# Value products of the last neighbourhood heads spread over other projections, and the high parts of the dilated values' operand copied into residue order

## The chip, the cores and the metric

The kernel runs on one core of a Trainium2 chip. The core has a matrix engine (TensorE, PE in the profile, its weight loads PEld), a vector engine (VectorE, DVE), a scalar engine (ScalarE, ACT), GpSimd (POOL) and SyncE (SP), which work side by side and wait for each other by semaphores; each runs its own instructions in the order in which they stand in the program. Matmul results go into PSUM, here eight banks of 128 partitions x 512 floats. The metric is the device time of one execution in microseconds (us); lower is better.

## What is computed

One layer of an encoder: a half-step feed-forward block, a mixing block, and a second half-step feed-forward block, each between two RMS norms, for 512 tokens of 1024 channels in float32. The change lies in the mixing block:

```
proj = h @ w_in[l]
qa, ka, va, qb, kb, vb, gate_a, gate_b = jnp.split(proj, splits, axis=-1)
ya = _neighbourhood_attention(qa, ka, va, na_rpb[l]) @ w_branch_a[l]
yb = _dilated_mixture(qb, kb, vb, slopes) @ w_branch_b[l]
merged = jax.nn.sigmoid(gate_a) * ya + jax.nn.sigmoid(gate_b) * yb
x = x + _rmsnorm(merged @ w_out[l], mix_post_g[l])
```

The neighbourhood attention has 8 heads of 64 channels, each query looking at a window of rows and columns of a 64-column grid. The dilated mixture has three groups of 4 heads: group 0 looks at neighbours at distance 1, group 1 at every 4th token, group 2 at every 16th. The three results of a head are mixed by their log-sum-exps.

## The kernel before

All products are made in three matmuls of reduced-precision parts: an operand is split into a high part (a cast, on ACT, line 116) and a low part (a subtraction, on DVE, line 117), and `mm3` (lines 207 to 209) sums high x high, high x low and low x high. `hn_hi` and `hn_lo` hold the normalised input of the mixing block, transposed: channels in the partitions, in NK = 8 chunks of 128, and 512 tokens in the free dimension. Weights come from HBM in pieces, are split likewise, and `take()` hands out the next piece. `bank()` gives a PSUM bank out of eight, `unit()` an SBUF buffer of 128 x 512 out of 46; who asks for one waits until its last user has gone.

The stretch of the mixing block in question runs so. `pair` makes the projections of the queries and of the keys of one pair of heads: 24 matmuls into a bank each, 5.7 us. After each projection it calls `step`, which takes the next entry from the list `pend` and issues it: the attention of earlier heads is interleaved with the projections in this way. There are four pairs of neighbourhood heads (`na_use`), then six pairs of dilated heads (`g_use`, pairs 0 and 1 of group 0, 2 and 3 of group 1, 4 and 5 of group 2). A pair of neighbourhood heads has three kinds of step: `sc` (scores of both heads, their minimum and exponential, lines 1109, 1116 and 1121), `na_tr` (transposes of one head's probabilities and their split, line 1143), and `na_pv` (value product of one head, line 1170, and then in `attend` a copy on ACT and an addition on DVE, line 1188, which read the bank; line 1186 is the copy). The table `plan` in `na_use` says which of them go together in one entry of `pend`: each inner tuple is one entry, so one entry is issued per projection. The last line of `plan`, that of the last pair, has eight entries, issued in pairs 1 to 4 of the dilated heads.

A pair of dilated heads is made into operands by `qk_parts` (lines 969 to 976, and 116, 117): of the queries a scaled high part on ACT (969) and a low part on DVE (970), of the keys a cast on ACT and a subtraction on DVE for each half, and copies to the other half of the partitions on DVE (975) and ACT (976). Scores of group 0 are made by `scores`, those of groups 1 and 2 by `scores_narrow` (lines 1081, 1085 and 1089): two matmuls to a bank, an addition of a table and two reductions on DVE, exponentials on ACT.

After the six pairs, `v_far` makes the values of groups 1 and 2: four accumulators of a bank each, over all eight chunks; for each chunk and each n of four, `mm3` with 128 tokens as the stationary operand and 512 columns of weight as the moving one. The 128 tokens are those of one residue modulo 4: `seen(1, .)` is a view of the chunk, every fourth token of 512, so PE's weight load reads it with a stride of 4. After every second chunk it calls `step` (twice after chunk 5), which issues the narrow scores that are left. Then `v_near` makes the values of group 0 (four products of 24 matmuls with 256 columns) and then come the gates.

The function `recopy` (line 990) is a plain copy on DVE or ACT; before the change it is used by the neighbourhood values, which are made from copies in another order of tokens, and by `v_near` for the tokens at the two ends.

A scheduler turns the code into one row of instructions for each engine; what is independent can stand in another order than in the code, by its estimates. An engine then keeps to its row.

Of the kernel before, what the change touches and what calls it, by code (L numbers as in the profile page):

```python
# [13 lines left out]
F32R = mybir.dt.float32r  # L14
# [6 lines left out]
P = 128  # L21
T = 512
D = 1024
NK = D // P
# [22 lines left out]
def block_kernel(ctx, tc, x, gains, weights, rpb_near, rpb_all, alibi0, alibi12, out):  # L47
    nc = tc.nc
# [12 lines left out]
    def unit(dt=F32, name="u"):  # L61
        return up.tile([P, 512], dt, tag="u", name=name)
# [9 lines left out]
    def bank(name="ps"):  # L72
        return pp.tile([P, 512], F32, tag="ps", name=name)
# [17 lines left out]
    hn_hi, hn_lo = Rows(), Rows()  # L91
# [88 lines left out]
    def cut(w, c, n):  # L180

        return [a[c // 512][:, c % 512:c % 512 + n] for a in w]

    def take(ahead=True):
        w = pieces.pop(state["take"])
        state["take"] += 1
        if ahead:
            fill(NPIECE - 1)
        return w
# [11 lines left out]
    def step(n=1):  # L201
        for _ in range(n):
            if pend:
                pend.popleft()()

    def mm3(o, sh, sl, mh, ml, start, stop, **kw):
        nc.tensor.matmul(o, sh, mh, start=start, stop=False, **kw)  # L207
        nc.tensor.matmul(o, sh, ml, start=False, stop=False, **kw)  # L208
        nc.tensor.matmul(o, sl, mh, start=False, stop=stop, **kw)  # L209
# [701 lines left out]
    def seen(kind, ap):  # L911

        if kind == "na":
            return ap.rearrange("p (r c) -> p c r", r=8)
        if kind == 0:
            return ap
        return ap.rearrange("p (i c) -> p c i", c=4)
# [24 lines left out]
    def shaped(dst, view):  # L942
        sh = view.shape
        if len(sh) == 2:
            return dst
        if len(sh) == 3:
            return dst.rearrange("p (a b) -> p a b", a=sh[1])
        return dst.rearrange("p (a b c) -> p a b c", a=sh[1], b=sh[2])

    def qk_parts(kind, pq, pk):  # L950


        if kind not in (1, 2):
            qh, ql, kh, kl = [unit(F32R, n) for n in "qqkk"]
            v = seen(kind, pq)
            qo = shaped(qh, v)
            nc.scalar.mul(qo, v, 0.125)
            nc.vector.scalar_tensor_tensor(shaped(ql, v), v, 0.125, qo.bitcast(F32), op0=ALU.mult, op1=ALU.subtract)
            for cols, v in order_k(kind, pk):
                split(shaped(kh[:, cols], v), shaped(kl[:, cols], v), v)  # L960
            return qh, ql, kh, kl
        heads = []
        for par in range(2):
            own = slice(par * 64, par * 64 + 64)
            other = slice(64 - par * 64, 128 - par * 64)
            q, kh, kl = unit(F32R, "q"), unit(F32R, "k"), unit(F32R, "k")
            v = seen(kind, pq[own])
            qo, qx = shaped(q[own], v), shaped(q[other], v)
            nc.scalar.mul(qo, v, 0.125)
            nc.vector.scalar_tensor_tensor(qx, v, 0.125, qo.bitcast(F32), op0=ALU.mult, op1=ALU.subtract)  # L970
            v = seen(kind, pk[own])
            for i, u in enumerate((kh, kl)):
                part = v[:, 2 * i:2 * i + 2]
                split(shaped(u[own, :256], part), shaped(u[own, 256:], part), part)
            nc.vector.tensor_copy(kh[other], kh[own].bitcast(F32))
            nc.scalar.copy(kl[other], kl[own].bitcast(F32))
            heads.append((q, kh, kl))
        return heads

    def v_parts(ps):  # L980
        v = unit(F32R)
        v4 = v.rearrange("p (h s d) -> p h s d", h=4, s=2)
        split(v4[:, :, 0, :], v4[:, :, 1, :], ps.rearrange("p (h d) -> p h d", h=4))
        return v4

    def recopy(dst, src, eng):
        if eng is nc.scalar:
            nc.scalar.copy(dst, src.bitcast(F32))
        else:
            nc.vector.tensor_copy(dst, src.bitcast(F32))  # L990
# [27 lines left out]
    def v_far():  # L1018

        acc = [bank() for _ in range(4)]  # L1020
        for k in range(NK):
            if k % 2 == 0:
                w = take()
            parts = [seen(1, a[:, k, :]) for a in (hn_hi, hn_lo)]
            for n in range(4):
                mm3(acc[n], parts[0][:, n], parts[1][:, n], *cut(w, (k % 2) * 512, 512), k == 0, k == NK - 1)
            if k % 2:
                step(2 if k == 5 else 1)
        vv = [[], []]
        for n in range(4):  # L1030
            for i in range(2):
                vv[i].append(v_parts(acc[n][:, i * 256:(i + 1) * 256]))
        return vv
# [196 lines left out]
    def mixing(g):  # L1230
# [9 lines left out]
        def load_tables(us, n, src):  # L1240
            def one(i):
                u = unit(name="table")
                nc.sync.dma_start(u, src[:, i * 512:(i + 1) * 512])
                us.append(u)
            for i in range(n):
                loads.append(lambda i=i: one(i))
# [16 lines left out]
        def na_sc(parts, h):  # L1263
            s4 = [sp.tile([P, 4, 1, 2], F32, tag="nast", name="nast", bufs=4) for _ in range(2)]
            pr = scores(parts, [table_of(na_tab[h // 2], n) for n in range(2)],
                        [lambda i, t=t: t[:, i, 0] for t in s4])
            for n in range(2):
                rc = sp.tile([P, 4], F32, tag="narc", name="narc", bufs=4)
                nc.vector.reciprocal(rc, s4[n][:, :, 0, 1])
                scale_probs(True, pr[n], lambda i: rc[:, i:i + 1])  # L1270
                hold["p", h + n] = pr[n]
# [7 lines left out]
        def na_use(p, pq, pk):  # L1279
            if p < 3:  # L1280
                load_tables(na_tab[p + 1], 3, bias_f[:, (p + 1) * 1536:(p + 2) * 1536])
            parts = qk_parts("na", pq, pk)
            sc = lambda: na_sc(parts, 2 * p)
            plan = (((sc,), (), ((na_tr, 0),)),
                    (((na_tr, 1),), (sc,), ((na_pv, 0),), ((na_pv, 1), (na_tr, 2))),
                    (((na_tr, 3),), (sc,)),
                    (((na_pv, 2),), ((na_pv, 3), (na_tr, 4)), ((na_tr, 5),), (sc,), ((na_pv, 4),),
                     ((na_pv, 5), (na_tr, 6)), ((na_tr, 7),), ((na_pv, 6), (na_pv, 7))))
            for group in plan[p]:
                pend.append(lambda group=group: [f() if callable(f) else f[0](f[1]) for f in group])  # L1290

# [51 lines left out]
        load_tables(na_tab[0], 3, bias_f[:, 0:1536])  # L1343
        v_na = v_proj_na()
        first_pairs(na_use, (0, 2), lambda: next(v_na))
        vva += next(v_na)
        g_post, g_pre = gain(g), gain(g + 1)
        pair(na_use, 2, 1)
        pair(na_use, 3, 1)
        load_tables(g_tab[0], 3, alibi0[:, :1536])  # L1350
        load_tables(g_tab[1], 3, alibi0[:, 1536:])
        load_tables(g_tab[2], 1, alibi12[:, :512])
        load_tables(g_tab[3], 1, alibi12[:, 512:])
        for j in range(6):
            pair(g_use, j, 1)
        pend.append(lambda: joint(1))
        vvb[1], vvb[2] = v_far()
        vvb[0] = v_near()
        step(len(pend))
# [26 lines left out]
        parts = {}  # L1386
# [108 lines left out]
        acc = o.acc["r"] + o.acc["q"], o.acc["c"] + o.acc["z"]  # L1495
# [276 lines left out]
```

## Time and profile before

| | us |
|---|---|
| median of 3 runs | 1077.44 (1077.13 to 1077.58) |
| the profiled execution | 1077.08 |
| its span | 1075.3 |
| DVE busy, share of the span | 78% |
| ACT busy, share of the span | 60% |

The profile is one execution of the program. A row of the timeline gives the start (us from the span's start), the duration, engine, line, operation, tiles out<-in and their shapes, and in brackets the idle time of the engine before it and who ended that. In the view of the waits a row names an engine's waiting instruction, the one that released it, and three figures: the sum of the waits, their number and the longest. A row of the chain of waits has a start, a duration and the engine with its line. A row of a group of instructions gives busy time and mean nanoseconds of one, then the idle time before them. A row of the windows gives the stretch, its length, the busy time of PE, PEld, DVE, ACT and POOL (with the number of instructions), the granted clock of TensorE as a share of the full one, the busy share of the DMA engines and GB/s.

In the stretch from 440 us to the gates, PE is idle for 0.39 us in all, by the windows:

```profile
440.00:500.56 60.56, 60.17 (x331) 50.30 (x329) 40.28 (x85) 33.37 (x69) 0.00 (x0) 1.00 0.26 83
500.56:502.52 1.96, 1.96 (x25) 1.82 (x25) 1.90 (x10) 1.96 (x7) 0.00 (x0) 1.00 0.02 8
502.52:528.00 25.48, 25.48 (x113) 25.12 (x113) 18.34 (x70) 20.37 (x70) 0.00 (x0) 1.00 0.26 84
528.00:541.50 13.50, 13.50 (x114) 13.48 (x113) 11.86 (x56) 11.06 (x42) 0.00 (x0) 1.00 0.16 42
```

The first row is the rest of the projections, with the steps of the last neighbourhood heads among them; the second the last scores of group 0; the third holds `v_far` and most of the narrow scores; the fourth the rest of `v_near`.

### The profile page before, as it was taken

How to read it: one execution, taken by the hardware profiler on the slowest of the kernel's cores; microseconds unless marked ns; L12 is line 12 of the kernel's file. 1: busy time of each engine (PE TensorE's matmuls, PEld its weight loads, DVE VectorE, ACT ScalarE, POOL GpSimd, SP SyncE). 2: the span in 40 equal slices, each digit the busy share in tenths (PEclk: the TensorE clock that was granted, in tenths of full speed). 3: DMA queues.
4: the chain of work that ended last, by engine and by line, in shares of the span. 5: the costliest groups of instructions: out<-in, count | busy, mean ns of one | idle time of the engine just before them, and what ended most of it. 6: DMA issues, size and time to landing. Idle time of an engine off the chain costs nothing.

```text
span 1075.3 us, 17988 instructions
## 1 busy us (share of the span) xinstructions
PE 1067.7 (99%) x6435; PEld 952.3 (89%) x6435; DVE 843.1 (78%) x1624; ACT 649.3 (60%) x1312; POOL 178.6 (17%) x247
## 2 busy tenths in 40 slices
PE   9999999999999999999999999999999999999997
PEld 7899999998888988888988888889899999998886
DVE  7988888878997566686777654777998888889985
ACT  7655665566684665566775651366665655666672
POOL 4111222013334000000000001133302111103301
PEclk9999999999999999999999999999999999999999
DMA  9989998469994454322232239566928767859962
GB/s 328 201 212 231 232 231 200 139 175 267 239 293 104 155 168 147 119 73 66 80 103 81 79 109 307 135 135 203 283 73 207 199 166 187 205 176 241 223 211 78
DMA packets 95724, 189.80 MB, mean 177 GB/s; under 512 B 24081, under 2 KB 26641, under 8 KB 95634
## 3 DMA queue, kind: packets, MB, share of 16 engines
q1 hardware_dynamic: 68320, 134.18, 37.0%
q0 software_dynamic: 24624, 54.01, 28.2%
q8 instruction: 50, 0.82, 0.3%
q10 hardware_dynamic: 2690, 0.46, 0.2%
q14 instruction: 40, 0.33, 0.1%
HBM read 183.58 MB, written 7.58 MB: 178 GB/s over the span
## 4 chain that ended last, share of the span: by engine, by line
PE 99%; DVE 0%; ACT 0%; issue 0%; DVEq 0%; ACTq 0%
PE q L209 11%; PE q L207 11%; PE q L208 11%; PE ps L207 11%; PE ps L209 11%; PE ps L208 10%; PE p L458 6%; PE p L460 3%; PE r L208 3%; PE r L209 3%; PE r L207 3%; PE c L207 2%; PE c L209 2%; PE c L208 2%; PE q L273 1%; PE ps L1143 1%
## 5 line engine op out<-in xcount | busy, mean ns | idle before, releaser
L117 DVE TENSOR_TENSOR w<-raw,w 128x512 fp32r<-128x512 f32 (+1 forms) x138 | 125.5, 914 | 93.3 <-ACT w L116 91.5
L116 ACT CAST w<-raw 128x512 fp32r<-128x512 f32 (+1 forms) x138 | 109.9, 802 | 94.7 <-PE ps L208 44.1
L207 PE MATMUL ps<-hn,w 128*128 128x512 f32 (+1 forms) x360 | 136.5, 379 | 0.4 <-DVE u L1188 0.4
L209 PE MATMUL ps<-hn,w 128*128 128x512 f32 (+1 forms) x360 | 134.5, 374 | 0.0
L208 PE MATMUL ps<-hn,w 128*128 128x512 f32 (+1 forms) x360 | 134.3, 373 | 0.0
L116 ACT CAST w<-t 128x512 fp32r<-128x512 f32 x160 | 97.4, 620 | 46.2 <-DVE t L413 28.7
L117 DVE TENSOR_TENSOR w<-t,w 128x512 fp32r<-128x512 f32 x160 | 109.2, 690 | 17.3 <-ACT w L116 15.1
L458 PE MATMUL p<-v,w 128*128 128x512 f32 x256 | 93.1, 397 | 0.0
L208 PE MATMUL q<-v,w 128*128 128x256 f32 x320 | 90.4, 283 | 0.0
L209 PE MATMUL q<-v,w 128*128 128x256 f32 x320 | 90.3, 283 | 0.0
L207 PE MATMUL q<-v,w 128*128 128x256 f32 x320 | 90.3, 283 | 0.0
L407 POOL DMA_DIRECT2D t<-in_weights_dram x40 | 35.0, 874 | 282.9 <-DVE w L117 94.1
L209 PE MATMUL q<-hn,w 128*128 128x256 f32 x288 | 81.6, 283 | 0.0
L208 PE MATMUL q<-hn,w 128*128 128x256 f32 x288 | 81.5, 283 | 0.0
L207 PE MATMUL q<-hn,w 128*128 128x256 f32 x288 | 81.3, 283 | 0.0
L209 PEld LDWEIGHTS ps<-hn,w 128*128 128x128 f32 x360 | 67.8, 188 | 12.7 <-DVE w L117 0.7
L207 PEld LDWEIGHTS ps<-hn,w 128*128 128x128 f32 x360 | 67.9, 189 | 11.9 <-DVE u L1188 0.6
L208 PEld LDWEIGHTS ps<-hn,w 128*128 128x128 f32 x360 | 67.9, 189 | 10.9
L460 PE MATMUL p<-v,w 128*128 128x256 f32 x256 | 71.7, 281 | 0.0
L207 PEld LDWEIGHTS q<-v,w 128*128 128x128 f32 x320 | 60.8, 190 | 0.3
L208 PEld LDWEIGHTS q<-v,w 128*128 128x128 f32 x320 | 60.9, 190 | 0.1
L207 PE MATMUL q<-w,a 128*128 128x512 f32 x156 | 60.9, 390 | 0.0
(328 smaller groups left out, 3046.6 us busy)
## 6 DMA issues: line engine op xcount, KB each, us to landing
raw<-in_weights_dram SPq DMA_DIRECT2D x90, 512.0 KB
t<-in_weights_dram SPq DMA_DIRECT2D x88, 256.0 KB
t<-in_weights_dram POOLq DMA_DIRECT2D x80, 256.0 KB, 5.9
w<-in_weights_dram SPq DMA_DIRECT2D x40, 256.0 KB
rows<-in_weights_dram SPq DMA_DIRECT2D x32, 256.0 KB
w<-in_weights_dram POOLq DMA_DIRECT2D x32, 256.0 KB, 5.8
tb<-in_weights_dram POOLq DMA_DIRECT2D x12, 512.0 KB, 7.3
rows<-in_weights_dram POOLq DMA_DIRECT2D x24, 256.0 KB, 11.1
```

The source lines that it names most:

```text
L116: nc.scalar.copy(hi, src)
L117: nc.vector.tensor_tensor(lo, src, hi.bitcast(F32), op=ALU.subtract)
L207: nc.tensor.matmul(o, sh, mh, start=start, stop=False, **kw)
L208: nc.tensor.matmul(o, sh, ml, start=False, stop=False, **kw)
L209: nc.tensor.matmul(o, sl, mh, start=False, stop=stop, **kw)
L273: nc.tensor.matmul(to, parts[j][part], hn_hi[:, k0 + j, 0:256], start=k0 + j + part == 0, stop=False, skip_group_check=True)
L407: nc.gpsimd.dma_start(t1, weights[gate][:, :512], accum_op=ALU.add)
L458: nc.tensor.matmul(o[key, j], w[:, k * P:(k + 1) * P], mv[i][k][2], start=start and k == 0, stop=False, skip_group_check=True)
L460: nc.tensor.matmul(acc, w[:, 512 + k * P:512 + (k + 1) * P], mv[i][k][0], start=False, stop=k == 3, skip_group_check=True)
L1143: nc.tensor.transpose(ps[:, i * P:(i + 1) * P], s, ident)
```

## The change

It has two parts. In `na_use`, the entries of the last pair are grouped anew. There are eight as before, and the steps keep their order but for `sc`, which moves from the fourth entry to the third; `na_tr(5)` goes into one entry with `na_pv(4)`, `na_pv(5)` and `na_tr(6)` have one each, `na_tr(7)` goes with `na_pv(6)`, and `na_pv(7)` is an entry by itself. In `v_far`, the high part of each chunk is copied on DVE into a `unit`, the four residues one after the other, and the two matmuls that take the high part as the stationary operand (lines 207 and 208) read it from there, 128 tokens side by side. The low part is read through the strided view as before. That makes eight copies of 128 x 512 (line 990). From line 1024 on, a line of the changed kernel has a number higher by 2 than that of before (1081 is 1083, 1089 is 1091, 1109 is 1111, 1116 is 1118, 1170 is 1172).

```diff
@@ v_far @@
             if k % 2 == 0:
                 w = take()
-            parts = [seen(1, a[:, k, :]) for a in (hn_hi, hn_lo)]
+            high, low = [seen(1, a[:, k, :]) for a in (hn_hi, hn_lo)]
+            u = unit(F32R)
+            recopy(shaped(u, high), high, nc.vector)
             for n in range(4):
-                mm3(acc[n], parts[0][:, n], parts[1][:, n], *cut(w, (k % 2) * 512, 512), k == 0, k == NK - 1)
+                mm3(acc[n], u[:, n * P:(n + 1) * P], low[:, n], *cut(w, (k % 2) * 512, 512), k == 0, k == NK - 1)
             if k % 2:
                 step(2 if k == 5 else 1)
@@ na_use @@
-                    (((na_pv, 2),), ((na_pv, 3), (na_tr, 4)), ((na_tr, 5),), (sc,), ((na_pv, 4),),
-                     ((na_pv, 5), (na_tr, 6)), ((na_tr, 7),), ((na_pv, 6), (na_pv, 7))))
+                    (((na_pv, 2),), ((na_pv, 3), (na_tr, 4)), (sc,), ((na_pv, 4), (na_tr, 5)), ((na_pv, 5),),
+                     ((na_tr, 6),), ((na_pv, 6), (na_tr, 7)), ((na_pv, 7),)))
```

How the rows of the engines change is shown at three places; names carry a number that tells buffers apart (ps a bank, u a unit, k and q the operands of scores, w weights, hn the input), and the shape is that of the output.

On PE, where the last scores of group 0 (line 1109) end and the dilated values begin, before:

```order
L1109 MATMUL ps_6046<-k_5501,q_5499 128x256
L1109 MATMUL ps_6046<-k_5502,q_5499 128x256
L1109 MATMUL ps_6046<-k_5501,q_5500 128x256
L207 MATMUL ps_6114<-w_5720,hn_4243 128x512
L208 MATMUL ps_6114<-w_5721,hn_4243 128x512
L209 MATMUL ps_6114<-w_5720,hn_4244 128x512
```

The same place of the changed kernel:

```order
L1111 MATMUL ps_6046<-k_5502,q_5499 128x256
L1111 MATMUL ps_6044<-k_5501,q_5500 128x256
L1111 MATMUL ps_6046<-k_5501,q_5500 128x256
L207 MATMUL ps_6114<-w_5735,u_6124 128x512
L208 MATMUL ps_6114<-w_5736,u_6124 128x512
L209 MATMUL ps_6114<-w_5735,hn_4244 128x512
```

The first dilated product follows the last score directly in both; now it reads `u_6124`, the copy of the first chunk, in place of `hn_4243`.

On DVE, from the last reductions of those scores on, where the operands of pair 5 are made, before:

```order
L1116 ISA u_6050,st_4364<-ps_6046,table_5392 128x256
L1116 ISA st_4364 128x1
L970 SCALAR_TENSOR_TENSOR q_6092<-ps_5933,q_6092 64x512
L117 TENSOR_TENSOR k_6093<-ps_6012,k_6093 64x256
L975 CAST k_6093<-k_6093 64x512
L117 TENSOR_TENSOR k_6094<-ps_6012,k_6094 64x256
L970 SCALAR_TENSOR_TENSOR q_6103<-ps_5933,q_6103 64x512
L117 TENSOR_TENSOR w_6170<-raw_6167,w_6169 128x1024
L117 TENSOR_TENSOR k_6104<-ps_6012,k_6104 64x256
L975 CAST k_6104<-k_6104 64x512
L1085 TENSOR_TENSOR low_6152<-ps_6149,table_5438 128x256
L117 TENSOR_TENSOR k_6105<-ps_6012,k_6105 64x256
```

The same place of the changed kernel:

```order
L1118 ISA u_6050,st_4364<-ps_6046,table_5392 128x256
L1118 ISA st_4364 128x1
L970 SCALAR_TENSOR_TENSOR q_6092<-ps_5933,q_6092 64x512
L117 TENSOR_TENSOR k_6093<-ps_6012,k_6093 64x256
L975 CAST k_6093<-k_6093 64x512
L117 TENSOR_TENSOR k_6094<-ps_6012,k_6094 64x256
L970 SCALAR_TENSOR_TENSOR q_6103<-ps_5933,q_6103 64x512
L117 TENSOR_TENSOR k_6104<-ps_6012,k_6104 64x256
L975 CAST k_6104<-k_6104 64x512
L990 CAST u_6124<-hn_4243 128x512
L990 CAST u_6138<-hn_4243 128x512
L117 TENSOR_TENSOR k_6105<-ps_6012,k_6105 64x256
```

The first two copies stand behind the reductions and behind the operands of pair 5; one weight split (`w_6170`) no longer stands between those.

On PE, further on, where the third pair of chunks of the dilated values ends, in the changed kernel:

```order
L209 MATMUL ps_6117<-w_5868,hn_4246 128x512
L1083 MATMUL ps_6268<-k_5783,q_5781 128x256 x2
L1083 MATMUL ps_6278<-k_5793,q_5792 128x256 x2
L1083 MATMUL ps_6287<-k_5794,q_5792 128x256 x2
L1083 MATMUL ps_6332<-k_5912,q_5911 128x256 x2
L1083 MATMUL ps_6341<-k_5913,q_5911 128x256 x2
L207 MATMUL ps_6406<-w_6015,hn_4243 128x256
```

In the kernel before the narrow scores stood apart, between the matmuls of the values:

```order
L1081 MATMUL ps_6247<-k_5782,q_5781 128x256 x2
L207 MATMUL ps_6114<-w_5936,hn_4245 128x512
L208 MATMUL ps_6114<-w_5937,hn_4245 128x512
L1081 MATMUL ps_6256<-k_5783,q_5781 128x256 x2
L209 MATMUL ps_6114<-w_5936,hn_4246 128x512
L207 MATMUL ps_6115<-w_5936,hn_4245 128x512
L208 MATMUL ps_6115<-w_5937,hn_4245 128x512
L1081 MATMUL ps_6266<-k_5793,q_5792 128x256 x2
```

Five narrow scores now stand together, each in a bank of its own, and the first product of `v_near` (`ps_6406`) comes next, ahead of the last pair of chunks of `v_far`. Outside the stretch from the last neighbourhood heads to the gates the rows of all engines are the same.

## The prediction

> **What bounds the kernel now.** I read the page's busy times and its chain first, then the waits of TensorE (PE) in the stretch that the change touches.
>
> ```profile
> PE 1067.7 (99%) x6435; PEld 952.3 (89%) x6435; DVE 843.1 (78%) x1624; ACT 649.3 (60%) x1312; POOL 178.6 (17%) x247
> ...
> PE 99%; DVE 0%; ACT 0%; issue 0%; DVEq 0%; ACTq 0%
> ```
>
> PE is busy in 99% of the span, and the chain that ended last is PE alone. So a microsecond in which PE stands still is paid in full, and one that another engine saves beside PE pays nothing. Between 380 and 545 us, the view of the waits has one line for PE, and the timeline shows where it lies:
>
> ```profile
> PE ps L207 <- DVE u L1188: 0.4, 1, 0.4
> ```
> ```profile
> 494.09 0.68 DVE L1188 TENSOR_TENSOR u<-ps,u 64x512 f32<-64x512 f32 x1
> ...
> 494.82 0.50 PE L207 MATMUL ps<-hn,w 128*128 128x512 f32 x1 [0.39 <-DVE u L1188]
> ```
>
> Pair 5's projection waits 0.39 us for a PSUM bank that VectorE (DVE) empties at the end of the last value product (`na_pv(7)`, popped together with `na_pv(6)`). This is all the idle time that the new plan can remove. The chain then runs without a gap into `v_far`:
>
> ```profile
> 500.56 1.96 PE ps L1109 x24
> ...
> 503.07 0.23 PE ps L208
> ...
> 509.66 0.23 PE ps L209
> ```
>
> The last scores of group 0 (1.96 us) end at 502.5, and the dilated value products start at once: their operands `hn` and `w` have long been there.
>
> **The change part by part.** *The plan.* `na_pv(7)` is alone now and lies inside an earlier projection; the bank is free long before: **−0.39 us**. The other moved steps: scores to `na_tr(6)` are three steps apart instead of two, and transposes to their value product at least one, as before. One step is a projection, 5.7 us (494.82 to 500.56), against 0.68 us for such an addition. That cover makes their cost nothing; where it failed, the price would be another 0.39. The steps moved issue no DMA and pass no load on SP's or POOL's queue.
>
> *The copies: a new wait.* Until now `L207` took `hn` itself; now it takes `u`, which DVE writes with eight new casts (line 990). DVE runs its instructions in the order written: the first copy stands behind the reductions of the last scores and behind the queries and keys of pair 5. These are the rows of before for what is queued there:
>
> ```profile
> 505.38 0.42 DVE L1116 CUSTOM_DVE_ANT_0 u<-ps,table 128x256 f32<-128x256 f32 x1
> ...
> 505.73 0.42 DVE L1116 CUSTOM_DVE_ANT_0 u<-ps,table 128x256 f32<-128x256 f32 x1
> ...
> 507.06 0.68 DVE L970 SCALAR_TENSOR_TENSOR q<-ps,q 64x512 fp32r<-64x512 f32 x1 [0.56 <-ACT q L969]
> 507.77 0.42 DVE L117 TENSOR_TENSOR k<-ps,k 64x256 fp32r<-64x256 f32 x1
> 508.22 0.42 DVE L975 CAST k<-k 64x512 fp32r<-64x512 f32 x1
> 510.53 0.42 DVE L117 TENSOR_TENSOR k<-ps,k 64x256 fp32r<-64x256 f32 x1 [1.88 <-ACT k L116]
> 511.14 0.69 DVE L970 SCALAR_TENSOR_TENSOR q<-ps,q 64x512 fp32r<-64x512 f32 x1 [0.20 <-ACT q L969]
> 512.22 1.23 DVE L117 TENSOR_TENSOR w<-raw,w 128x1024 fp32r<-128x1024 f32 x1 [0.38 <-ACT w L116]
> 513.48 0.43 DVE L117 TENSOR_TENSOR k<-ps,k 64x256 fp32r<-64x256 f32 x1
> 513.94 0.42 DVE L975 CAST k<-k 64x512 fp32r<-64x512 f32 x1
> 514.39 0.42 DVE L1085 TENSOR_TENSOR low<-ps,table 128x256 f32<-128x256 f32 x1
> ```
>
> In before DVE has done this part at 514.36, 11.84 us after PE began `v_far`. Nobody on PE needed it; now PE does. A copy itself:
>
> ```profile
> L990 DVE CAST u<-hn 128x384 fp32r<-128x384 f32 x8 | 4.3, 534 | 0.0
> L990 DVE CAST u<-hn 128x128 fp32r<-128x128 f32 x8 | 2.3, 289 | 0.0
> ```
>
> 245 ns more for 256 more elements: 0.96 ns each, so 128x512 takes an estimated 534 + 123 = 657 ns, 0.66 us. The wait, from both sides. At the least DVE does, after the last score, only what it must: two reductions at a pitch of 0.35 (505.38 to 505.73), then from these rows 0.71 + 0.45 + 0.45 + 0.46 + 0.71 + 0.46 + 0.45 (queries and keys of both halves, from one start to the next), and the copy: **5.0 us**. At the most it is as late as in before: 11.84 + 0.66 = **12.5 us**. Which one it is nearer to depends on ScalarE (ACT), which stands between:
>
> ```profile
> 501.14 1.04 ACT L116 CAST w<-raw 128x1024 fp32r<-128x1024 f32 x1
> ...
> 506.43 0.59 ACT L969 ACTIVATE q<-ps 64x512 fp32r<-64x512 f32 x1
> 506.92 0.35 ACT L116 CAST k<-ps 64x256 fp32r<-64x256 f32 x1
> 507.18 0.51 ACT L1121 ACTIVATE u<-u,st 128x256 f32<-128x256 f32 x1
> ...
> 510.14 0.35 ACT L116 CAST k<-ps 64x256 fp32r<-64x256 f32 x1
> ```
>
> In the new order the projection ends near 500.2 (0.39 sooner) and PE is through the scores at about 502.1. A weight piece is still cast by ACT first (to about 501.5) and split by DVE (1.23 by the row at 512.22, to about 502.8); a reduction later, at about 503.2, ACT has eight exponentials (0.49 each: six of them fill 507.18 to 510.14) and a query copy and a key cast between (0.49 and 0.26 by the starts above), 4.7 us. So the second key cast, which in before starts at 510.14, starts at about 507.9. From that cast to the end of the queries and keys DVE took 4.22 us (to 514.36); the weight split of 1.23 and its wait of 0.38 stand behind the copy now, which leaves 2.6. DVE then copies from 510.5 to 511.2, and PE has waited since 502.1: **+9.1 us**, between the bounds and from the nearest rows of both engines. The other seven copies (4.6 us of DVE) lie beside twelve matmuls each (2.8 us) and cost nothing; if they had no cover, each could be late by its own 0.66.
>
> *Banks.* The order now puts five narrow scores together behind the third pair of chunks, and then the first product of `v_near`, with four banks beside the four accumulators. The fifth score needs the first one's bank, `v_near` the second one's. From the nearest rows:
>
> ```profile
> 522.30 0.42 DVE L1085 TENSOR_TENSOR low<-ps,table 128x256 f32<-128x256 f32 x1
> 522.64 1.22 DVE L117 TENSOR_TENSOR w<-raw,w 128x1024 fp32r<-128x1024 f32 x1
> 523.77 0.28 DVE L1089 CUSTOM_DVE_ANT_0 u<-ps,low 128x128 f32<-128x128 f32 x1
> 523.98 0.29 DVE L1089 CUSTOM_DVE_ANT_0 u<-ps,low 128x128 f32<-128x128 f32 x1
> ```
>
> The first bank is free two additions (0.34 pitch) and two reductions (0.21 pitch) after its score, about 1.2 us; PE has three scores (0.24 each) to fill it: 0.5. The next waits for a weight split (1.13 from 522.64 to 523.77) and two more reductions, less one score: 1.3. Together **+1.8 us**; bounds 0 (DVE is ahead, or the buffers are free) and 2.9 (both waits with another split's 1.1).
>
> *Contiguous loads.* The stationary operand of 64 of the 96 matmuls is no longer read with a stride:
>
> ```profile
> L207 PEld LDWEIGHTS ps<-w,hn 128*128 128x128 f32 x32 | 10.0, 312 | 0.1
> ```
> ```profile
> L208 PEld LDWEIGHTS ps<-hn,w 128*128 128x128 f32 x8 | 1.5, 188 | 0.3
> ```
> ```profile
> 495.32 0.24 PE ps L208
> ...
> 500.33 0.23 PE ps L209
> ```
>
> The first two rows are loads in `v_far` and in a projection: 312 against 188 ns. They run beside the matmul before, so the pitch tells what they cost: 503.07 to 509.66 is 28 steps at 235.4 ns; 495.32 to 500.33, 22 at 227.7. 7.6 ns × 64 = **−0.5 us**. Bounds: 0, and 64 × 124 = 7.9 us gained if a load were paid in full, which the pitch contradicts.
>
> *The clock after the wait.* PE never stood for 9 us before, but at both ends of the program one sees what its clock does:
>
> ```profile
> 1069.00:1070.00 1.00, 0.28 (x2) 0.00 (x0) 0.14 (x1) 0.62 (x2) 0.00 (x0) 1.00 1.00 373
> ...
> 1071.00:1072.00 1.00, 0.00 (x0) 0.00 (x0) 1.00 (x3) 0.00 (x0) 0.00 (x0) 0.78 0.00 0
> 1072.00:1073.00 1.00, 0.00 (x0) 0.00 (x0) 0.57 (x2) 0.00 (x0) 0.00 (x0) 0.50 0.69 234
> ```
> ```profile
> 1.18 3.17 PE warm L1549 x7
> ...
> 6.51 0.34 PE warm L1549
> ...
> 7.29 0.22 PE warm L1549
> ```
>
> PE's work ends at about 1069.3, and the granted clock (third figure from the end) is 0.78 in the window from 1071 and 0.50 in the next: it fell after some 2.3 us of standing. At the start a matmul takes 0.45 (3.17 for seven), 0.34 at 6.51 and 0.22 at 7.29: about 5.3 us (1.18 to 6.51) at half rate, in which half the work is lost, 2.65. A wait of 9 us is longer than 2.3, so I take **+2.7 us**; bounds 0 and 2.7. The Trainium skill, "TensorE: Matmul & The Clock Gate", section "Part 1: The HAM clock gate", gives an idle window of about 3.4 us for the fall and 3.4 us of work for the return; by its figure the loss would be an estimated 1.7 and the time 1088.8. The trace agrees with a halving, though it fell after 2.3 and took 5.3 to return.
>
> *The sum.* −0.4 + 9.1 + 1.8 − 0.5 + 2.7 = +12.7. The profiled execution took 1077.08 us (span 1075.3), the median of the runs 1077.44, 0.03% more, so I keep its base: 1077.1 + 12.7 = **1089.8 us**.
>
> **The rivals.** *Clock holds:* as above without the 2.7: 1087.1. For it: matmuls run on both sides and only one gap lies between; against it: the rows at the end of the span.
>
> *Short wait:* ACT's and DVE's work on the scores runs ahead, and the wait is 5.0: 1085.7. Against it: the key cast at 510.14, which stands behind eight exponentials.
>
> *Long wait:* DVE keeps the pace of before, 12.5: 1093.2. For it: exactly these instructions ended at 514.36; against it: a split has left the queue, and the scores start sooner.
>
> *Other side: the copy is ready in time.* If DVE gets to the first copy by 502.1, when PE is through the scores, there is no wait, no fall of the clock and a gain of 0.4 + 0.5: 1076.2, which is no measurable change. It decides at the place of the first copy in DVE's row: 9.1 us of queue would have to go, and the last two reductions there need those very scores, so it can't be earlier than 5.0 unless the copy went ahead of them.
>
> *Loads are the bound after all:* 7.9 gained instead of 0.5: 1082.4. Against it: the pitch of 235 ns under loads of 312.
>
> **How the numbers follow.** Forecast 1089.8: 53%. Clock holds 20%, short wait 12%, long wait 10%, copy in time 3%, loads the bound 1%, loads the bound and the copy in time (1077.1 − 0.4 − 7.9 = 1068.8) 1%. The range goes from 1083.0 (5.0 of wait, no fall of the clock, all else as summed) to 1094.3 (12.5 of wait, banks 2.9). A measurement of this kernel tells apart about 0.2%, 2.2 us: slower 0.96, within 0.03, faster 0.01.
>
> **What would show it.** In the changed profile: a wait of PE at `L207 ps<-w,u` near 502 for DVE's copy (line 990), 9 us long; a granted clock under 1 for some microseconds behind it; the wait on the last value product gone; PE loads of `u` at 188 and of `hn` still at 312; two short waits at the narrow scores (0.5 and 1.3); the gates, which follow, 10 to 13 us later. I am wrong if DVE's copy of the first chunk starts before the last scores' reductions, if ACT's exponentials are not in front of the key cast, or if the clock stays at 1.00 behind a wait of several microseconds.

## The result and the profile after

| | us | ratio to before |
|---|---|---|
| before, median of 4 runs | 1077.45 (1077.13 to 1077.58) | |
| changed, median of 4 runs | 1090.03 (1088.98 to 1090.18) | 1.0115, 95% interval 1.010 to 1.013 |
| the changed kernel's profiled execution (span) | 1088.98 (1087.2) | |

The profiled execution is the fastest of the four, 11.9 us above before's (1077.08). Of the eleven runs of `plan_only`, below, three took 1309 to 3760 us, the profiled one among them; its ratio is of the other eight. The page of the changed kernel says that TensorE (PE) has been busy about as long as before in a longer span; the view of its waits from 380 us to the gates says what fills the rest:

```profile
PE 1068.5 (98%) x6435; PEld 949.6 (87%) x6435; DVE 847.1 (78%) x1632; ACT 649.2 (60%) x1312; POOL 178.5 (16%) x247
```
```profile
PE ps L207 <- DVE u L990: 9.8, 1, 9.8
PE ps L207 <- DVE st L1091: 1.1, 1, 1.1
PE ps L1083 <- DVE st L1091: 0.6, 1, 0.6
```

The wait on the last value product is gone; three new ones have come. The first lies between the last scores and the first dilated product (timeline of PE, the changed kernel):

```profile
499.55 1.69 PE L1111 MATMUL ps<-k,q 64*128 64x256 f32 x24
511.00 0.79 PE L207 MATMUL ps<-w,u 128*128 128x512 f32 x1 [9.76 <-DVE u L990]
...
532.80 0.47 PE L1083 MATMUL ps<-k,q 128*128 128x256 f32 x2 [0.64 <-DVE st L1091]
534.36 0.36 PE L207 MATMUL ps<-w,hn 128*128 128x256 f32 x1 [1.09 <-DVE st L1091]
```

PE is through the scores at 501.24 and stands until 511.00. What VectorE (DVE) does meanwhile, from the same kernel's timeline:

```profile
501.24 1.23 DVE L117 TENSOR_TENSOR w<-raw,w 128x1024 fp32r<-128x1024 f32 x1 [2.85 <-ACT w L116]
...
508.04 0.42 DVE L117 TENSOR_TENSOR k<-ps,k 64x256 fp32r<-64x256 f32 x1 [1.20 <-ACT k L116]
508.65 0.69 DVE L970 SCALAR_TENSOR_TENSOR q<-ps,q 64x512 fp32r<-64x512 f32 x1 [0.20 <-ACT q L969]
509.43 0.43 DVE L117 TENSOR_TENSOR k<-ps,k 64x256 fp32r<-64x256 f32 x1
509.89 0.42 DVE L975 CAST k<-k 64x512 fp32r<-64x512 f32 x1
510.33 1.14 DVE L990 CAST u<-hn 128x512 fp32r<-128x512 f32 x2
```

It splits a weight, reduces the scores, makes the operands of pair 5, waiting for ScalarE (ACT) on the way, and only then copies. The wait of 1.20 us is for ACT's second key cast, which stands behind the exponentials in ACT's row:

```profile
507.65 0.35 ACT L116 CAST k<-ps 64x256 fp32r<-64x256 f32 x1
```

While PE stands and after it, the windows of the changed kernel (the third figure from the end is the granted clock):

```profile
505.00:505.50 0.50, 0.00 (x0) 0.00 (x0) 0.47 (x3) 0.50 (x3) 0.00 (x0) 0.66 0.65 262
...
515.25:515.50 0.25, 0.25 (x2) 0.16 (x2) 0.00 (x0) 0.00 (x0) 0.00 (x0) 0.69 0.00 0
515.50:516.00 0.50, 0.50 (x4) 0.45 (x3) 0.00 (x0) 0.00 (x0) 0.00 (x0) 1.00 0.00 0
```

The clock falls to half at 505.2, 3.9 us after PE stopped, and comes back at 515.4, 4.4 us after it started again. In these 4.4 us half the work is lost, 2.2 us. Put together: start of `v_far` at 511.00 instead of 502.52, that is 9.76 of wait less 1.28 by which PE came sooner; 1.73 of waits at the banks; 2.2 of the clock. That is 12.4. From the first dilated product to the first product of the gates (511.00 to 553.33, before 502.45 to 541.46) the changed kernel takes 42.3 us instead of 39.0; without these waits and the clock that would be 38.4, some 0.6 less than before (see "The loads"). So 11.8 is accounted for, and 11.9 was measured.

### The profile page after: what moved, and what is told of

Its sections match the earlier page's. It is cut to its first block, busy times and chain, and to the rows that moved or that the text cites. A ratio compares the mean times of both kernels' runs of the same rounds, so it can differ in the third digit from the quotient of the medians.

```text
span 1087.2 us, 18001 instructions
## 1 busy us (share of the span) xinstructions
PE 1068.5 (98%) x6435; PEld 949.6 (87%) x6435; DVE 847.1 (78%) x1632; ACT 649.2 (60%) x1312; POOL 178.5 (16%) x247
## 4 chain that ended last, share of the span: by engine, by line
PE 98%; ACT 1%; DVE 1%; issue 0%; DVEq 0%; ACTq 0%
PE q L209 11%; PE q L207 11%; PE q L208 11%; PE ps L207 11%; PE ps L209 10%; PE ps L208 10%; PE p L458 6%; PE p L460 3%; PE r L209 3%; PE r L208 3%; PE r L207 3%; PE c L209 2%; PE c L207 2%; PE c L208 2%; PE q L273 1%; PE ps L1145 1%
## 5 line engine op out<-in xcount | busy, mean ns | idle before, releaser
L208 PEld LDWEIGHTS ps<-hn,w 128*128 128x128 f32 x360 | 67.9, 189 | 10.9
```

## The experiments

The theory: the copies' own time is nearly nothing, and the place of the first one in DVE's row is nearly all. Each ratio below is to runs of the kernel before on the same chip.

**Each part alone.** `plan_only` has the new table `plan` and the old `v_far`; `copies_only` the new `v_far` and the old table.

> The new plan with the old v_far: both parts through the strided view, no copies. Theory (copies make the wait): no wait of TensorE from 440 us to the gates, granted clock 1.00 throughout, the last scores of group 0 begin near 499.6 as in the changed kernel (before: 500.6), median about 1076.4 (1.0 us under before: 0.39 of the bank wait, and some 0.7 because the two heads' score matmuls alternate without a break, 1.69 us each against 2.13 and 1.96). Rival (regrouping the steps is what crowds VectorE): a wait of several us also without the copies, median above 1080.

> The copies with the old plan. Theory: the same wait for the first copy, 9 to 12 us long (VectorE starts the last reductions some 0.7 us later than in the changed kernel, and TensorE comes 1.0 later too, so near 9.5), the clock falls and costs about 2.2, the two bank waits of 1.7 stay if the scheduler puts five narrow scores together here too; median 1090.5 to 1091.5. Rival (the plan makes the wait): at most 1 us of waits, median below 1080.

`plan_only`: median 1075.59, ratio 0.9984 (0.9975 to 0.9994). Its profile is that of `plan_only2`, the same kernel:

> The plan alone once more, for its profile. As before: no wait of TensorE between 440 us and the gates, clock 1.00, scores of 1.69 us for each of group 0's two steps, the last ones begun near 499.6, loads of the dilated values at 305 to 312 ns with a pitch of 0.235; median 1075.4 to 1076.

1075.86, ratio 0.9986 (0.9977 to 0.9995); no wait of PE between 380 us and the gates. `copies_only`: 1092.2, ratio 1.0138 (1.0125 to 1.0152), 0.7 above the range that was given, as the first wait is 10.9 us where some 9.5 were expected:

```profile
PE ps L207 <- DVE u L990: 10.9, 1, 10.9
...
PE ps L207 <- DVE u L1190: 0.4, 1, 0.4
```

The two waits at the banks, 1.1 and 0.6, are those of the changed kernel. So the copies bring all three new waits and the plan none: by itself it is worth 1.6 us. The two timelines of PE show more of that than the bank wait of 0.39, first `copies_only` (old plan), then `plan_only2` (new plan), each with the two steps of group 0's scores:

```profile
491.66 0.38 PE L1111 MATMUL ps<-k,q 64*128 64x256 f32 x1
491.97 0.62 PE L1172 MATMUL ps<-u 128*128 128x256 f32 x3
492.52 1.69 PE L1111 MATMUL ps<-k,q 64*128 64x256 f32 x23
494.60 0.50 PE L207 MATMUL ps<-hn,w 128*128 128x512 f32 x1 [0.39 <-DVE u L1190]
...
500.26 2.03 PE L1111 MATMUL ps<-k,q 64*128 64x256 f32 x24
```
```profile
493.17 1.69 PE L1109 MATMUL ps<-k,q 64*128 64x256 f32 x24
...
500.45 1.69 PE L1109 MATMUL ps<-k,q 64*128 64x256 f32 x24
```

With the old plan the first scores are broken by three matmuls of the value product, and the last ones take 2.03 us; with the new one both take 1.69. (That they begin at 500.45 and not near 499.6 is no lasting difference: the steps before stand 0.9 us later too, 493.17 against 492.27 in the changed kernel.) In the order of before these last 24 matmuls go six by six into one bank after another (the last six into `ps_6046`), in the changed one they alternate between two (at the end `ps_6044` and `ps_6046`), each on 64 of the 128 rows. That alternating ones overlap more is how I read the 0.3 us; it was not tried by itself.

**The place of the copy.** `far_copy` makes a chunk's copy as the change does. In `ahead4` the first four are written before the projections of pair 5, the others in the loop as before; in `ahead4_start`, which the diff shows, those stand at the start of `v_far`; in `ahead4_rest0` the last four chunks are not copied.

```diff
     def v_far():
+        for k in range(len(far), NK):
+            far_copy(k)
...
         for j in range(6):
+            if j == 5:
+                for k in range(4):
+                    far_copy(k)
             pair(g_use, j, 1)
```

> The changed kernel with the first four copies written ahead of the projections of pair 5, the other four where they were. Theory (it is the place of the first copy in VectorE's row, not the copy's own time): no wait at the first dilated product, no fall of the clock, 11.9 us of the wait and clock terms gone, the bank waits at the narrow scores left (0 to 2.5), median 1076 to 1078.5. Rival (copies cost by their own duration, 8 x 0.6 us): 4 to 5 us above the kernel with the plan alone.

1080.13, ratio 1.0027 (1.0017 to 1.0036). The wait of 9.8 us is gone, but the forecast of 1078.5 at most was missed by the next one of its kind; the waits of PE, then DVE's timeline and the windows, of `ahead4`:

```profile
PE ps L207 <- DVE u L990: 2.1, 1, 2.1
PE ps L1091 <- DVE st L1099: 0.4, 1, 0.4
```
```profile
515.44 1.22 DVE L117 TENSOR_TENSOR w<-raw,w 128x1024 fp32r<-128x1024 f32 x1 [0.60 <-ACT w L116]
516.59 1.14 DVE L990 CAST u<-hn 128x512 fp32r<-128x512 f32 x2
```
```profile
517.00:518.00 1.00, 0.75 (x3) 0.70 (x4) 1.00 (x4) 0.00 (x0) 0.00 (x0) 0.85 0.64 78
518.00:519.00 1.00, 1.00 (x4) 0.82 (x3) 1.00 (x10) 0.70 (x4) 0.00 (x0) 0.50 0.69 242
...
521.00:522.00 1.00, 1.00 (x6) 0.87 (x5) 0.00 (x0) 0.49 (x4) 0.00 (x0) 0.94 0.00 0
```

The fifth copy stands behind the narrow scores' reductions and a weight split; PE waits 2.1 us for it, and even that made the clock fall.

> As ahead4, and the other four copies written at the start of the dilated values instead of each before its own chunk, so that they stand in VectorE's row ahead of the narrow scores' reductions. Theory (what is left in ahead4, a wait of 2.1 us for the fifth copy and the fall of the clock behind it, comes from that copy's place behind the narrow scores): no wait for a copy anywhere, granted clock 1.00, at most 0.5 us of bank waits, median 1074.9 to 1075.9, that is the kernel with the plan alone less up to 0.5 for the contiguous loads. Rival (eight copies hold units or VectorE so long that something else is late): 1077 or more.

> As ahead4, but the last four chunks are read through the strided view, as in the kernel before: four copies, not eight. Theory: no wait for a copy, clock 1.00, bank waits at the narrow scores 0 to 1, median 1075.2 to 1076.4. Rival (ahead4's wait at the fifth chunk was for the weights' split or a bank, not for the copy): a wait of 1 us or more stays at the same place.

`ahead4_start`: 1075.15, ratio 0.9977 (0.9969 to 0.9986); `ahead4_rest0`: 1075.29, ratio 0.9981 (0.9972 to 0.9990). Neither has a wait of PE in the stretch. The windows of `ahead4_start` from 500 to 545:

```profile
500.00:545.00 45.00, 45.00 (x272) 40.98 (x272) 36.05 (x141) 35.06 (x127) 0.00 (x0) 1.00 0.25 76
```

PE is busy for all of it at full clock. The same eight copies with which the kernel was 14 us and more slower than the plan alone cost nothing here, and the waits at the banks are gone too; most of the narrow scores now stand apart in PE's row. This is the fastest of the kernels tried that compute the layer. It beats the plan alone too: `plan_only2` ran on the same chip in the same series (median 1075.86 against 1075.15), and ten of the eleven runs of `ahead4_start` are shorter than all eleven of `plan_only2`.

**The other engine.** `copies_act` gives the eight copies to ACT (`nc.scalar` in place of `nc.vector`).

> The changed kernel with the eight copies on ScalarE instead of VectorE. In its row the first copy stands behind the last key cast of pair 5, which in the changed kernel ended at 510.3 after a wait for VectorE. Theory (the copy is late because it stands behind the operands of pair 5, on whichever of the two engines, and those pass to and fro between the two): a wait of 9 to 10.5 us at the first dilated product, median 1089 to 1091. Rival (VectorE's load is the cause): a wait of 5 us or less, below 1085.

1088.41, ratio 1.010 (1.0086 to 1.0114). PE's longest wait and ACT's timeline:

```profile
PE ps L207 <- ACT u L988: 10.2, 1, 10.2
```
```profile
510.35 0.37 ACT L116 CAST k<-ps 64x256 fp32r<-64x256 f32 x1 [0.49 <-DVE k L117]
510.74 2.10 ACT L988 CAST u<-hn 128x512 fp32r<-128x512 f32 x2
```

The copy starts within 0.4 us of where DVE began it, behind the last key cast of pair 5. So it is the row of pair 5's operands, which passes to and fro between both engines, that the copy has to stand behind, and not something of DVE alone. (The median is just under the range that was given; behind the copy PE waits for only 0.2 us more in this stretch, instead of the 1.7 at the banks.)

**The clock.** `warm36` and `warm30` put matmuls whose result is overwritten where PE stands idle:

```diff
         acc = [bank() for _ in range(4)]
+        for _ in range(36):
+            nc.tensor.matmul(acc[0], hn_hi[:, 0, :P], hn_hi[:, 0, :], start=True, stop=True)
```

> The changed kernel with 36 matmuls of 128x512 whose result is overwritten, put between the last scores and the first dilated product (8.2 us at 0.228 each). VectorE's row is unchanged, so the copy still ends near 511.0 and TensorE waits some 1.5 us instead of 9.8. Theory (the fall of the clock is a cost of its own): granted clock 1.00 from 511 on, first products at 0.23 instead of 0.43, the kernel 2.2 us faster than the changed one (profile about 1086.8, median 1087 to 1088). Rival (half rate behind the wait is something else, such as the loads of the fresh copies): no change from 1089 to 1090.

> As warm36 with 30 such matmuls (6.8 us instead of 8.2): TensorE stands for about 2.8 us before the first dilated product. Theory (the clock falls once TensorE has been idle for most of some 3 us, as behind ahead4's waits of 0.4 and 2.1): in the profile a fall to half behind the wait or none, depending on how the gap lies in time; where it falls, about 4 us at half rate and 2 us lost, so median 1087 to 1089.5. Rival (only a wait of 4 us or more makes it fall): 1087.1 as with 36, clock 1.00.

`warm36`: 1087.13, ratio 1.0094 (1.0079 to 1.0109), the first product at 511.46 after a wait of 1.38 us, about as late as before, but at full clock. `warm30`: 1089.33, ratio 1.0112 (1.0098 to 1.0126), a wait of 2.7 us. The windows behind the wait, `warm36` first, and one more of `warm30`:

```profile
511.00:512.00 1.00, 0.54 (x2) 0.49 (x3) 0.97 (x3) 0.00 (x0) 0.00 (x0) 1.00 0.00 0
512.00:513.00 1.00, 1.00 (x6) 0.87 (x6) 0.41 (x1) 0.56 (x1) 0.00 (x0) 1.00 0.00 0
```
```profile
511.00:512.00 1.00, 0.00 (x0) 0.00 (x0) 0.99 (x3) 0.29 (x1) 0.00 (x0) 0.80 0.00 0
512.00:513.00 1.00, 0.97 (x2) 0.83 (x3) 0.92 (x2) 0.01 (x1) 0.00 (x0) 0.50 0.00 0
...
515.00:516.00 1.00, 1.00 (x5) 0.86 (x5) 0.00 (x0) 0.00 (x0) 0.00 (x0) 0.99 0.00 0
...
535.50:536.00 0.50, 0.50 (x5) 0.50 (x4) 0.50 (x2) 0.00 (x0) 0.00 (x0) 0.50 0.65 147
```

The same late copy costs some 2 us more where the clock falls (`warm36` against the changed kernel: ratios 0.0021 apart, 2.3 us, with overlapping intervals; the windows are what shows it). The last row is a second fall in `warm30`, behind the two bank waits of 0.64 and 1.09 us, to half from 535.5 to 538.9. Its profiled execution (1090.6, the slowest of four) pays for both, so its time is no price of the 2.7 us alone. The same two bank waits left the clock at full in the changed kernel, `copies_only` and `warm36`.

**The loads.** `no_stride` takes 128 neighbouring tokens of both parts in place of every fourth, without copies; it leaves out the order by residues.

> The new plan without copies, the 128 tokens of both parts taken side by side from the chunk instead of every fourth: this leaves out the reordering into residues, so the dilated values belong to other tokens, with the same number and shape of matmuls. It measures what strided loads cost by themselves. Theory of the prediction (a strided load costs 7.6 ns of pitch): pitch of the dilated products 0.228 instead of 0.235, 96 x 7.6 ns = 0.7 us under the plan alone, median 1074.9 to 1075.4. Rival 1 (loads paid in full): 96 x 124 ns = 12 us less, near 1064. Rival 2 (the pitch in this stretch is another cost, the loads are hidden entirely): pitch stays 0.235, same time as the plan alone.

1074.08, ratio 0.997 (0.9959 to 0.9982), lower than the range that was given. The pitch (the time from the start of one matmul to that of the next), from the chain of waits: `plan_only2` (both parts strided) with 30 steps between these rows, `ahead4_start` (the low part strided) with 20, `no_stride` with 24:

```profile
502.70 0.24 PE ps L208
...
509.76 0.23 PE ps L209
```
```profile
502.20 0.23 PE ps L208
...
506.85 0.24 PE ps L208
```
```profile
502.39 0.24 PE ps L208
...
507.85 0.23 PE ps L209
```

235.3, 232.5 and 227.5 ns. In the pitch all strides cost 96 x 7.8 = 0.75 us, and the copies of the high part win 96 x 2.8 = 0.27 of it. The pitch is not all. From the first dilated product to the first of the gates `plan_only2` takes 38.7 us, `ahead4_start` 38.1 and `no_stride` 37.4, none with a wait: 0.57 and 1.33 less. Much of the rest lies where a dilated product follows a narrow score, first `plan_only2`, then `no_stride`:

```profile
514.33 0.24 PE ps L1081 x2
514.57 0.35 PE ps L207
```
```profile
513.56 0.23 PE ps L1081 x2
513.79 0.23 PE ps L207
```

With a strided load the product takes 0.35 there, without one 0.23. `plan_only2` has five such places in `v_far`, all at 0.35 (the kernel before, which takes 39.0 us, has eight); of seven in `ahead4_start` only the three are so long where the low part's product, line 209, comes first; `no_stride` has none.

## Why the prediction was right, point by point

- **The wait, +9.1: 9.76 measured**, at the place and with the releaser that were named. Its parts: PE came at 501.24, not 502.1; ACT's second key cast starts at 507.65, behind the eight exponentials, where the estimate had 507.9; the copy starts at 510.33 against 510.5 and PE goes on at 511.00 against 511.2. A copy takes 0.57 instead of 0.66 (1.14 for two). `ahead4` and `copies_act` show why: another place takes the wait away, another engine does not.
- **Bank waits, +1.8: 1.73**, 0.64 and 1.09 where 0.5 and 1.3 were forecast.
- **The clock, +2.7: 2.2.** The fall was right. The way back took 4.4 us, not the 5.3 of the start of the program; behind like waits it took 4.7 in `copies_only` and 5.5 in `copies_act`, so the size was within what it can be. (At the start of the program the windows give a clock of 1.00; there the half rate rests on the matmuls' 0.45 against 0.22 us.) The rival in which the clock holds is refuted by the windows, and `warm36` shows the time without the fall.
- **The plan, −0.4: −1.3 in the profile, −1.6 by its own runs.** The mechanism was right as far as it went, and the term was too small: the prediction looked for waits of PE only. The score matmuls' different durations (1.96 against 1.69 us) stood in the timelines of before, but I took them as fixed.
- **The loads, −0.5: some −0.6 in the stretch, but not as it was worked out.** The loads of `u` took 188 ns and those of `hn` 309, as was said. Taking 64 of 96 loads as two thirds of the gain in pitch was too simple: of the 23 ns that a triple of matmuls gains without strides, one strided load left in it takes back 15, so the pitch gives −0.27. The rest of what `ahead4_start` wins (0.57) lies largely at the narrow scores, which the prediction had not looked at. That the term came out is luck.
- **The cover of the other seven copies** held for all of them in the changed kernel, as was said; in `ahead4` it failed for the fifth. That the long wait itself lets DVE catch up in the changed kernel is how I read this.

The errors of the terms are +0.7 (wait), −0.1 (banks), −0.5 (clock), −0.9 (plan) and −0.1 (loads). The first and the fourth are mostly one thing: PE came 0.9 us sooner than forecast and waited that much longer for a copy that was done when it was forecast, to 0.2 us. What is left is about the 0.8 by which the forecast of 1089.8 lies above the profiled execution. That it is within 0.2 of the median is luck: the other three runs took 0.9 to 1.2 us longer than the profiled one, and no trace shows why. The other side, a copy that is ready in time, is what `ahead4_start` is: there it took the copies out of the place that the change gave them.

## What to carry to other kernels

Where an engine is the bound, an operand that was ready gets a producer only if that producer's place in its engine's row is before the consumer's turn: read the row ahead of it, not the duration of the operation. A copy of 0.6 us cost some 12 us behind a full row (9.8 of wait and 2.2 of clock) and nothing ahead of it, and moving it to another engine with the same work ahead did not help. Price the idle time of TensorE with the clock that follows: in `warm30` two waits of 0.6 and 1.1 us close together were enough for a fall. Measure a change of the loads over the whole stretch and not by the pitch alone, and look in the timeline for the same group of matmuls at two durations: its order is worth something too.

## What the runs showed of the hardware

- **The clock goes by stretches of 3.4 us.** Once fallen, it stood at half for 3.4 us in `ahead4` (517.7 to 521.1) and both times in `warm30`; for 10.2, three times 3.4, in the changed kernel (505.2 to 515.4); and for 13.7, four times, in `copies_only` (504.3 to 518.0) and `copies_act` (503.8 to 517.4). In the 3.4 us that ended with a fall, PE had stood for 1.7 us (the second fall of `warm30`), 2.0 (`copies_only`), 2.1 (`copies_act`), 2.3 (the first of `warm30`), 2.5 (`ahead4`) and 3.4 (the changed kernel). Counting on from the fall in steps of 3.41, the bank waits of the changed kernel lie 0.3 in one stretch and 1.4 in the next, and the clock held. So the place of a wait in these stretches decides, and not its length alone; what happens between 1.4 and 1.7 us no run here shows. The way back took 3.0 (`warm30`) to 5.5 us (`copies_act`) of work. The Trainium skill, "TensorE: Matmul & The Clock Gate", section "Part 1: The HAM clock gate", tells of a free-running window of 3.4 us; these multiples fit with it, though PE had stood for only half of one when the clock fell the second time in `warm30`.
- **A strided stationary operand** makes a load of 312 ns in place of 188 (128 x 128), of which 7.8 ns show in the pitch when every load is strided, and some 0.12 us in a product directly behind a narrow score (0.35 in place of 0.23).
- **A strided copy** costs the two engines differently: with every fourth element read, 128x512 took 0.57 us on DVE (1.14 for two) and 1.05 on ACT (2.10 for two).
